# Second expert product: groups taken in neighbouring pairs, one branch for a token half around both products

## Chip, cores, metric

One core of one Trainium2 chip. The metric is the device time of one execution in microseconds; an execution also has a span, from its first to its last instruction.

## What is computed

Two blocks follow each other. The first mixes 256 tokens of width 2048; the second mixes them again and then adds a layer of experts. The change lies in the last step of that layer:

```python
act = jax.nn.gelu(jnp.einsum('thkd,td->thk', u_sel, xb))
w = (gb * act)
v_sel = expert_v[idb]
return jnp.einsum('thk,thkd->td', w, v_sel)
```

Each token takes 8 x 16 of 16384 experts; its output is the sum of their rows of `expert_v` (2048 wide), each by its weight `w`. Afterwards a last norm is taken over each token.

## The kernel before

The kernel doesn't gather rows by token. It keeps a dense table `a_dram` of weights, expert by token (zero where a token didn't choose an expert), and multiplies it with the whole of `expert_v`. It first sorts the 16384 experts into four classes: used by the first 128 tokens alone, by both halves, by the second 128 tokens alone, by nobody. `idx` holds the sorted order and `bnd` the three bounds `s1`, `e0`, `e1` between the classes (L1475 to L1514). On the inputs of the reference, its own choice of the top 16 gives classes of 3733, 6461, 3748 and 2442 experts, so `s1` = 3733, `e0` = 10194 and `e1` = 13942.

The last stage (L1525 to L1656) has its order written out by hand (`tc.manual_schedule()`, L1602). The sorted experts are cut into 64 groups of 256 (two tiles `kk` of 128). A group is loaded by four indirect DMAs on GpSimd's queue, in `v_load` and `a_load`: two 1 MB tiles `vraw` and two parts of `araw`. `v_split` (L1561) then splits each fp32 value into a high and a low part: ScalarE copies (`vh`, `ah`), VectorE subtracts (`vl`, `al`). A tile of `v` is split in two halves of 1024 columns, so a group has four half buffers of `vh` and four of `vl`; the pools hold 12 of each, three groups. `vraw` has six buffers, three groups too.

`v_mm(i, t)` (L1584) multiplies one group with one token half `t`: 24 matmuls of 512 columns (2 tiles, 4 column blocks, 3 part products), accumulated in 8 PSUM banks that stay open over all groups. For both halves a group needs two such products. A product is left out when the whole group holds no expert of that half, by branches on TensorE's sequencer (L1624 to L1629):

```python
if i < NGR - 1:
    with tc.If(e1 > lo):
        with tc.If(e0 > lo):
            v_mm(i, 0)
        with tc.If(s1 < hi):
            v_mm(i, 1)
```

Every `If` is built with an other path that waits until all matmuls issued before are done, and then raises TensorE's semaphore by what the left-out matmuls would have raised it. ScalarE waits on that semaphore before it writes a part buffer again.

The groups are taken in the order `gro` (L1541), which spreads the classes: positions 0 to 2 need both halves, position 3 is a group of unused experts with no product (an empty group), position 4 needs both, 5 the second half alone, 6 the first half alone, 7 is empty, 8 needs the second half alone, and so on. In the loop (L1612) position `i` first puts `v_split(i + 2)` on ScalarE and VectorE and the loads of `i + 4` on GpSimd, then the products of `i`. The last position (L1630) always takes both products, and the final norm and the stores follow.

Of the kernel before, what the change touches and what calls it, by code (L numbers as in the profile page):

```python
# [6 lines left out]
F32 = mybir.dt.float32  # L7
F32R = mybir.dt.float32r
# [57 lines left out]
def model(tc, I, out):  # L66
    nc = tc.nc
    V, S, T, PO = nc.vector, nc.scalar, nc.tensor, nc.gpsimd
    es = ExitStack()
    with es:  # L70
# [50 lines left out]
        def load(n):  # L121
            for hf in range(2):
                load_half(n, hf)
# [243 lines left out]
        with ExitStack() as b1:  # L367
            w_ = b1.enter_context(tc.tile_pool(name="work1", bufs=1))
# [439 lines left out]
            for u in range(4):  # L808
                t = H("xr")
                xr.append(t)  # L810
                if u < 2:
                    f = rawp.tile([128, 1024], F32, name="raw", tag="raw")
                    h, l = whp.tile([128, 1024], F32R, name="wh"), wlp.tile([128, 1024], F32R, name="wl")
# [89 lines left out]
            late = []  # L903
# [9 lines left out]
        with ExitStack() as b2:  # L913
            hb2 = b2.enter_context(tc.tile_pool(name="hb2", bufs=8, reuse_waits="tile"))
            w_ = b2.enter_context(tc.tile_pool(name="work2", bufs=1, reuse_waits="tile"))
# [205 lines left out]
        with ExitStack() as bt:  # L1121
            w_ = bt.enter_context(tc.tile_pool(name="topk", bufs=1, reuse_waits="tile"))
# [167 lines left out]
            n = len(units) + 1  # L1290
# [245 lines left out]
        w_ = es_d.enter_context(tc.tile_pool(name="vph", bufs=1, reuse_waits="tile"))  # L1536
        arow = a_dram.rearrange("p j t -> (p j) t")
        KG = 2
        NV = 12
        NGR = NT // KG  # L1540
        gro = [(i * 23 + 55) % NGR for i in range(NGR)]  # L1541
        gro[0], gro[7] = gro[7], gro[0]
        raw, ar, sv, sa = {}, {}, {}, {}

        def ix(i, kk):
# [3 lines left out]
        def v_load(i):  # L1549
            raw[i] = []  # L1550
            for kk in range(KG):
                f = w_.tile([128, 2048], F32, name="vraw", tag="vraw", bufs=6)
                PO.indirect_dma_start(f, None, I["v"], ix(i, kk))  # L1553
                raw[i].append(f)

        def a_load(i):
            ar[i] = w_.tile([128, KG, 256], F32, name="araw", tag="araw", bufs=4)
            for kk in range(KG):
                PO.indirect_dma_start(ar[i][:, kk], None, arow, ix(i, kk))  # L1559

        def v_split(i, late=False):  # L1561
            h = w_.tile([128, KG, 256], F32R, name="ah", tag="ah", bufs=3)
            l = w_.tile([128, KG, 256], F32R, name="al", tag="al", bufs=3)
            sa[i] = (h, l)
            sv[i] = []

            def a_split():
                f = ar.pop(i)
                S.activation(h, f, AF.Copy)
                V.tensor_sub(l, f, h.bitcast(F32))  # L1570

            if not late:
                a_split()
            for f in raw.pop(i):
                for hf in range(2):
                    q = slice(hf * 1024, hf * 1024 + 1024)
                    wh, wl = (w_.tile([128, 1024], F32R, name=n, tag=n, bufs=NV) for n in ("vh", "vl"))
                    S.activation(wh, f[:, q], AF.Copy)  # L1578
                    V.tensor_sub(wl, f[:, q], wh.bitcast(F32))  # L1579
                    sv[i].append((wh, wl))  # L1580
            if late:
                a_split()

        def v_mm(i, t, last=False):  # L1584
            ah, al = (x[:, :, t * 128:t * 128 + 128] for x in sa[i])

            def one(kk, d, stop):
                wh, wl = (w[:, d % 2 * 512:d % 2 * 512 + 512] for w in sv[i][kk * 2 + d // 2])
                T.matmul(ps[t][d], ah[:, kk], wh, start=False, stop=False)  # L1589
                T.matmul(ps[t][d], ah[:, kk], wl, start=False, stop=False)  # L1590
                T.matmul(ps[t][d], al[:, kk], wh, start=False, stop=stop)  # L1591

            if last:
                for d in range(4):
                    for kk in range(KG):
                        one(kk, d, kk == KG - 1)
            else:
                for kk in range(KG):
                    for d in range(4):
                        one(kk, d, False)  # L1600
# [3 lines left out]
        for i in range(3):  # L1604
            v_load(i)
            a_load(i)
        s1, e0, e1 = (T.value_load(bnd[0:1, i:i + 1], min_val=0, max_val=NT * 128) for i in range(3))
        for i in range(2):
            v_split(i, late=i == 0)
        v_load(3)  # L1610
        a_load(3)
        for i in range(NGR):  # L1612
            if i + 2 < NGR:
                v_split(i + 2)
            if i + 4 < NGR:
                v_load(i + 4)
                a_load(i + 4)
            if i + 4 == NGR:
                gl = w_.tile([128, 2048], F32, name="gl", tag="vraw", bufs=6)
                nc.sync.dma_start(gl, I["last_g"])  # L1620
                ys = [w_.tile([128, 2048], F32, name="y", tag="vraw", bufs=6) for _ in range(2)]
            lo = gro[i] * KG * 128
            hi = lo + KG * 128
            if i < NGR - 1:  # L1624
                with tc.If(e1 > lo):
                    with tc.If(e0 > lo):
                        v_mm(i, 0)
                    with tc.If(s1 < hi):  # L1628
                        v_mm(i, 1)  # L1629
            else:  # L1630
                S.preload_act_table_set("sqrt_and_others")
                sq8 = pers.tile([128, 2, 4], F32, name="sq8")
                rf = pers.tile([128, 2], F32, name="rf")
                ov = out.rearrange("(t p) d -> p t d", p=128)
                for t in range(2):
                    v_mm(i, t, last=True)
                    y = [ys[t][:, d * 512:d * 512 + 512] for d in range(4)]
                    g = [gl[:, d * 512:d * 512 + 512] for d in range(4)]
                    sq = w_.tile([128, 512], F32, name="sq", tag="sq", bufs=2)
                    for d in range(4):  # L1640
                        S.activation(sq, ps[t][d], AF.Square, accum_out=sq8[:, t, d:d + 1])  # L1641
                        if d < 3:
                            V.tensor_mul(y[d], ps[t][d], g[d])
                    r = rf[:, t:t + 1]
                    V.tensor_reduce(r, sq8[:, t], axis=AX.X, op=OP.add)  # L1645
                    S.activation(r, r, AF.Sqrt, scale=1.0 / D_MODEL, bias=eps)  # L1646
                    V.reciprocal(r, r)  # L1647
                    S.activation(y[1], y[1], AF.Copy, scale=r)
                    V.scalar_tensor_tensor(y[3], ps[t][3], r, g[3], op0=OP.mult, op1=OP.mult)  # L1649
                    nc.sync.dma_start(ov[:, t, 3 * 512:4 * 512], y[3])  # L1650
                    nc.scalar.dma_start(ov[:, t, 512:1024], y[1])
                    for c in (0, 2):
                        V.tensor_scalar(y[c], y[c], r, None, op0=OP.mult)  # L1653
                        (nc.scalar if c else nc.sync).dma_start(ov[:, t, c * 512:(c + 1) * 512], y[c])  # L1654
            sv.pop(i)
            sa.pop(i)  # L1656
    return


# [104 lines left out]
```

## Time and profile before

| | us |
|---|---|
| runs, median of 3 | 2616.54 (2615.02 to 2618.34) |
| profiled execution, its time | 2615.54 |
| its span | 2613.8 |
| last stage, first to last product matmul | 2133.1 to 2605.0 of the span |
| TensorE busy in the span | 2531.6 (97%) |
| VectorE busy | 1935.7 (74%) |
| ScalarE busy | 1491.1 (57%) |
| GpSimd busy | 708.6 (27%) |

Between the span and the execution's own time lie 1.7 us. Matmuls overlap one another in the trace: what one costs in a row of them is the distance between starts, not its duration. Times in the rows further down are counted from the span's start. Engines are PE (TensorE), PEld (its weight loads), DVE (VectorE), ACT (ScalarE), POOL (GpSimd), and PEq is TensorE's sequencer.

### The profile page before, as it was taken

The numbers are of one execution on the slowest core, as the hardware profiler recorded it, in microseconds if no ns is written. First come the engines' busy times: TensorE is split into PE (matmuls) and PEld (weight loads), VectorE is DVE, ScalarE is ACT, GpSimd is POOL, SyncE is SP. The second block draws the span as 40 slices with busy tenths as digits, with TensorE's granted clock in tenths as the row PEclk, the third lists the DMA queues.
The fourth block names the chain that finished last, engine by engine and source line by source line (L and its number), as shares of the span: only waits on it lengthen the run. The fifth ranks groups of instructions, "written<-read, shape, count | busy, mean of one in ns | idle before, by whom it ended". The sixth has DMA issues, their size and how long they took to land. (4 is left out here: it accounts for less than half of the span.)

```text
span 2613.8 us, 38685 instructions
## 1 busy us (share of the span) xinstructions
PE 2531.6 (97%) x14650; PEld 2155.8 (82%) x14650; DVE 1935.7 (74%) x2671; ACT 1491.1 (57%) x2179; POOL 708.6 (27%) x419
## 2 busy tenths in 40 slices
PE   8999999999999999999998999999999999999998
PEld 7878878888888888888887788888888877777776
DVE  7988877676556555776889988888987448767676
ACT  7666665555544544555544766666455446656565
POOL 0450111000000000001446321211322248767773
PEclk9999999999999999999999999999999999999999
DMA  6444424555554455555555577667999859988885
GB/s 222 164 165 148 162 100 145 189 172 175 169 169 166 166 187 186 184 193 195 173 197 177 191 252 242 228 229 254 354 367 329 302 202 365 350 319 324 321 309 208
DMA packets 173540, 584.80 MB, mean 224 GB/s; under 512 B 17440, under 2 KB 50976, under 8 KB 156832
## 3 DMA queue, kind: packets, MB, share of 16 engines
q1 hardware_dynamic: 114336, 411.88, 45.9%
q0 software_dynamic: 24576, 151.01, 15.7%
q10 hardware_dynamic: 34432, 19.27, 2.5%
q8 instruction: 126, 2.06, 0.3%
q14 instruction: 70, 0.57, 0.1%
HBM read 536.48 MB, written 45.61 MB: 223 GB/s over the span
## 5 line engine op out<-in xcount | busy, mean ns | idle before, releaser
L238 PE MATMUL acc<-a,wh 128*128 128x512 f32 x3106 | 1112.2, 399 | 0.6 <-DVE y L248 0.6
L239 PE MATMUL acc<-a,wl 128*128 128x256 f32 x3106 | 878.5, 283 | 16.6 <-DVE wl L118 12.4
L238 PEld LDWEIGHTS acc<-a,wh 128*128 128x128 f32 x3106 | 585.4, 189 | 128.9 <-PE acc L236 0.9
L118 DVE TENSOR_TENSOR wl<-raw,wh 128x1024 fp32r<-128x1024 f32 x372 | 463.2, 1247 | 231.2 <-ACT wh L117 228.0
L117 ACT ACTIVATE wh<-raw 128x1024 fp32r<-128x1024 f32 x414 | 437.3, 1058 | 310.2 <-PE acc L238 191.0
L239 PEld LDWEIGHTS acc<-a,wl 128*128 128x128 f32 x3106 | 589.1, 190 | 25.1 <-DVE wl L118 15.2
L118 POOL TENSOR_TENSOR wl<-raw,wh 128x1024 fp32r<-128x1024 f32 x42 | 113.0, 2691 | 1079.3 <-ACT wh L117 1038.9
L118 POOL TENSOR_TENSOR wl<-ring,wh 128x1024 fp32r<-128x1024 f32 x70 | 204.5, 2921 | 544.6 <-ACT wh L117 514.5
L117 ACT ACTIVATE wh<-ring 128x1024 fp32r<-128x1024 f32 x248 | 259.9, 1054 | 143.6 <-PE acc L238 97.7
L1579 DVE TENSOR_TENSOR vl<-vraw,vh 128x1024 fp32r<-128x1024 f32 x256 | 296.6, 1221 | 19.3 <-ACT vh L1578 14.2
L118 DVE TENSOR_TENSOR wl<-ring,wh 128x1024 fp32r<-128x1024 f32 x178 | 233.4, 1317 | 59.8 <-ACT wh L117 58.5
L238 PE MATMUL acc<-ax,wh 128*128 128x512 f32 x720 | 264.9, 406 | 11.4 <-ACT wh L822 7.3
L1589 PE MATMUL o<-vh,ah 128*128 128x512 f32 x648 | 256.2, 395 | 18.4 <-PEq L1628 7.2
L1591 PE MATMUL o<-vh,al 128*128 128x512 f32 x648 | 252.5, 390 | 2.6 <-DVE al L1570 2.6
L1590 PE MATMUL o<-vl,ah 128*128 128x512 f32 x648 | 252.2, 389 | 0.0
L1578 ACT ACTIVATE vh<-vraw 128x1024 fp32r<-128x1024 f32 x256 | 248.9, 1044 | 0.0
L239 PE MATMUL acc<-ax,wl 128*128 128x256 f32 x720 | 209.2, 291 | 5.3 <-DVE wl L118 3.1
L247 ACT ACTIVATE y<-acc 128x512 f32<-128x512 f32 x161 | 95.3, 593 | 204.3 <-PE acc L236 188.2
L248 DVE TENSOR_TENSOR y<-y,acc 128x512 f32<-128x512 f32 x161 | 110.1, 685 | 115.8 <-ACT y L247 114.9
L1559 POOL DMA_INDIRECT araw<-a_dram,idx x128 | 178.5, 1394 | 47.5 <-issue 38.1
L1553 POOL DMA_INDIRECT vraw<-in_v_dram,idx x128 | 159.2, 1244 | 78.4 <-DVE vl L1579 40.3
L238 PEld LDWEIGHTS acc<-ax,wh 128*128 128x128 f32 x720 | 138.1, 192 | 40.8 <-ACT wh L822 7.3
(516 smaller groups left out, 4044.1 us busy)
## 6 DMA issues: line engine op xcount, KB each, us to landing
raw<-in_w_dram SPq DMA_DIRECT2D x278, 512.0 KB, 4.2
ring<-in_uT_dram SPq DMA_DIRECT2D x248, 512.0 KB, 5.1
raw<-in_wo_dram SPq DMA_DIRECT2D x64, 512.0 KB, 4.4
raw<-in_wq_dram SPq DMA_DIRECT2D x32, 512.0 KB, 4.2
g_dram<-gst ACTq DMA_DIRECT2D x32, 512.0 KB, 7.4
G<-g_dram SPq DMA_DIRECT2D x32, 512.0 KB, 7.6
xs<-y SPq DMA_DIRECT2D x19, 512.0 KB, 3.9
Xr<-xs SPq DMA_DIRECT2D x19, 512.0 KB, 9.3
```

The source lines that it names most:

```text
L117: S.activation(h[:, q], f[:, q], AF.Copy)
L118: (PO if (n, hf) in POOL_SUB else V).tensor_sub(l[:, q], f[:, q], h[:, q].bitcast(F32))
L238: T.matmul(acc[:, j], wh[:, js], xx, start=f, stop=False)
L239: T.matmul(acc[:, j, 0], wl[:, js], xx[:, 0], start=False, stop=False)
L248: V.tensor_add(y, y, acc[:, :, 0])
L1553: PO.indirect_dma_start(f, None, I["v"], ix(i, kk))
L1559: PO.indirect_dma_start(ar[i][:, kk], None, arow, ix(i, kk))
L1578: S.activation(wh, f[:, q], AF.Copy)
L1579: V.tensor_sub(wl, f[:, q], wh.bitcast(F32))
L1589: T.matmul(ps[t][d], ah[:, kk], wh, start=False, stop=False)
L1590: T.matmul(ps[t][d], ah[:, kk], wl, start=False, stop=False)
L1591: T.matmul(ps[t][d], al[:, kk], wh, start=False, stop=stop)
```

## The change

The 64 groups are taken as 32 pairs of neighbours (512 sorted experts), in the order `two`. For a pair `u`, `u + 1` an outer branch asks whether the pair holds a used expert. Inside, one branch asks for the first token half and holds the products of both groups (the second under a branch of its own), and one asks for the second half in the same way, so the order of a full pair is (u, first half), (u + 1, first half), (u, second half), (u + 1, second half). The splits of the next pair stand ahead of the products but for the second tile of its second group, which stands behind them; `vh` and `vl` get 14 half buffers, `ah` and `al` four in place of three. The second group's own test against `e1` is gone.

```diff
@@ -1536,10 +1536,11 @@
         w_ = es_d.enter_context(tc.tile_pool(name="vph", bufs=1, reuse_waits="tile"))
         arow = a_dram.rearrange("p j t -> (p j) t")
         KG = 2
-        NV = 12
+        NV = 14
         NGR = NT // KG
-        gro = [(i * 23 + 55) % NGR for i in range(NGR)]
-        gro[0], gro[7] = gro[7], gro[0]
+        two = [(i * 11 + 27) % (NGR // 2) for i in range(NGR // 2)]
+        two[0], two[8] = two[8], two[0]
+        gro = [p * 2 + j for p in two for j in range(2)]
         raw, ar, sv, sa = {}, {}, {}, {}
 
         def ix(i, kk):
@@ -1558,26 +1559,28 @@
             for kk in range(KG):
                 PO.indirect_dma_start(ar[i][:, kk], None, arow, ix(i, kk))
 
-        def v_split(i, late=False):
-            h = w_.tile([128, KG, 256], F32R, name="ah", tag="ah", bufs=3)
-            l = w_.tile([128, KG, 256], F32R, name="al", tag="al", bufs=3)
-            sa[i] = (h, l)
-            sv[i] = []
-
+        def v_split(i, tiles=range(KG), late=False):
             def a_split():
                 f = ar.pop(i)
+                h, l = sa[i]
                 S.activation(h, f, AF.Copy)
                 V.tensor_sub(l, f, h.bitcast(F32))
 
-            if not late:
-                a_split()
-            for f in raw.pop(i):
+            if tiles[0] == 0:
+                sa[i] = tuple(w_.tile([128, KG, 256], F32R, name=n, tag=n, bufs=4) for n in ("ah", "al"))
+                sv[i] = []
+                if not late:
+                    a_split()
+            for kk in tiles:
+                f = raw[i][kk]
                 for hf in range(2):
                     q = slice(hf * 1024, hf * 1024 + 1024)
                     wh, wl = (w_.tile([128, 1024], F32R, name=n, tag=n, bufs=NV) for n in ("vh", "vl"))
                     S.activation(wh, f[:, q], AF.Copy)
                     V.tensor_sub(wl, f[:, q], wh.bitcast(F32))
                     sv[i].append((wh, wl))
+            if tiles[-1] == KG - 1:
+                raw.pop(i)
             if late:
                 a_split()
 
@@ -1605,29 +1608,44 @@
             v_load(i)
             a_load(i)
         s1, e0, e1 = (T.value_load(bnd[0:1, i:i + 1], min_val=0, max_val=NT * 128) for i in range(3))
+        def load(i):
+            if i < NGR:
+                v_load(i)
+                a_load(i)
+
         for i in range(2):
             v_split(i, late=i == 0)
-        v_load(3)
-        a_load(3)
-        for i in range(NGR):
-            if i + 2 < NGR:
-                v_split(i + 2)
-            if i + 4 < NGR:
-                v_load(i + 4)
-                a_load(i + 4)
-            if i + 4 == NGR:
-                gl = w_.tile([128, 2048], F32, name="gl", tag="vraw", bufs=6)
-                nc.sync.dma_start(gl, I["last_g"])
-                ys = [w_.tile([128, 2048], F32, name="y", tag="vraw", bufs=6) for _ in range(2)]
-            lo = gro[i] * KG * 128
-            hi = lo + KG * 128
-            if i < NGR - 1:
+        load(3)
+        load(4)
+        for u in range(0, NGR, 2):
+            if u + 2 < NGR:
+                v_split(u + 2)
+                load(u + 5)
+                v_split(u + 3, range(1))
+            lo = gro[u] * KG * 128
+            mid, hi = lo + KG * 128, lo + 2 * KG * 128
+            if u + 2 < NGR:
                 with tc.If(e1 > lo):
                     with tc.If(e0 > lo):
-                        v_mm(i, 0)
+                        v_mm(u, 0)
+                        with tc.If(e0 > mid):
+                            v_mm(u + 1, 0)
                     with tc.If(s1 < hi):
-                        v_mm(i, 1)
+                        with tc.If(s1 < mid):
+                            v_mm(u, 1)
+                        v_mm(u + 1, 1)
+                v_split(u + 3, range(1, 2))
+                load(u + 6)
+                if u + 4 == NGR:
+                    gl = w_.tile([128, 2048], F32, name="gl", tag="vraw", bufs=6)
+                    nc.sync.dma_start(gl, I["last_g"])
+                    ys = [w_.tile([128, 2048], F32, name="y", tag="vraw", bufs=6) for _ in range(2)]
             else:
+                with tc.If(e0 > lo):
+                    v_mm(u, 0)
+                with tc.If(s1 < mid):
+                    v_mm(u, 1)
+                i = u + 1
                 S.preload_act_table_set("sqrt_and_others")
                 sq8 = pers.tile([128, 2, 4], F32, name="sq8")
                 rf = pers.tile([128, 2], F32, name="rf")
@@ -1652,8 +1670,9 @@
                     for c in (0, 2):
                         V.tensor_scalar(y[c], y[c], r, None, op0=OP.mult)
                         (nc.scalar if c else nc.sync).dma_start(ov[:, t, c * 512:(c + 1) * 512], y[c])
-            sv.pop(i)
-            sa.pop(i)
+            for i in range(u, u + 2):
+                sv.pop(i)
+                sa.pop(i)
     return
```

The built program is the same up to TensorE's first branch of the stage. Behind it the order differs on ScalarE, at two places. In the names, `vh_`, `ah_` are the high parts written, `vraw_`, `araw_` the loaded tiles; in brackets are the semaphores waited for (DMASW: a load, DVE: VectorE, PE: TensorE).

The first place is ScalarE where the products of an empty position are passed. Before, around position 3 (`ah_20905` is position 4, `ah_20983` position 5):

```order
L1569 ACTIVATE ah_20905<-araw_20773 128x512 [waits DMASW2_49,DMASW3_49,DVE_49,PE_49]
L1578 ACTIVATE vh_20909<-vraw_20769 128x1024 [waits DMASW0_49,DVE_49,PE_49]
L1578 ACTIVATE vh_20913<-vraw_20769 128x1024
L1578 ACTIVATE vh_20917<-vraw_20771 128x1024 [waits DMASW1_49]
L1578 ACTIVATE vh_20921<-vraw_20771 128x1024
L1625 UNCONDITIONAL_BRANCH
L1569 ACTIVATE ah_20983<-araw_20851 128x512 [waits DMASW6_49,DMASW7_49,DVE_49,PE_49]
```

Each position waits for TensorE once, at its start, for the position three before it.

After, around the first empty pair (positions 6 and 7; `vh_21206` and `vh_21210` are the second tile of position 7, `ah_21221` to `vh_21237` position 8, `ah_21248` to `vh_21365` position 9):

```order
L1579 ACTIVATE vh_21206<-vraw_20933 128x1024 [waits DMASW5_49,DVE_49,PE_49]
L1579 ACTIVATE vh_21210<-vraw_20933 128x1024
L1628 UNCONDITIONAL_BRANCH
L1566 ACTIVATE ah_21221<-araw_21063 128x512 [waits DMASW3_49,DMASW2_49]
L1579 ACTIVATE vh_21225<-vraw_21059 128x1024 [waits DMASW0_49]
L1579 ACTIVATE vh_21229<-vraw_21059 128x1024
L1579 ACTIVATE vh_21233<-vraw_21061 128x1024 [waits DMASW1_49]
L1579 ACTIVATE vh_21237<-vraw_21061 128x1024
L1566 ACTIVATE ah_21248<-araw_21090 128x512 [waits DMASW7_49,DMASW6_49]
L1579 ACTIVATE vh_21252<-vraw_21086 128x1024 [waits DMASW4_49]
L1579 ACTIVATE vh_21256<-vraw_21086 128x1024
L1579 ACTIVATE vh_21361<-vraw_21088 128x1024 [waits DMASW5_49,DVE_49,PE_49]
```

ScalarE now waits for TensorE once in a pair, at the second tile of the pair's second group: `vh_21206` waits for the end of the whole pair of positions 4 and 5, and all of positions 8 and 9 stand behind it.

The second place is the start of the stage on ScalarE. After (`ah_20702` is position 0, `ah_20722` position 1):

```order
L1579 ACTIVATE vh_20704<-vraw_20654 128x1024 [waits DMASW0_49]
L1579 ACTIVATE vh_20708<-vraw_20654 128x1024
L1579 ACTIVATE vh_20712<-vraw_20656 128x1024 [waits DMAHW6_49,DMAHW0_49,DMAHW7_49,DMASW1_49,DVE_49]
L1579 ACTIVATE vh_20716<-vraw_20656 128x1024 [waits PE_49]
L1566 ACTIVATE ah_20702<-araw_20658 128x512 [waits DMASW3_49,DMASW2_49]
L1566 ACTIVATE ah_20722<-araw_20665 128x512 [waits DMASW7_49,DMASW6_49]
```

Before, the order of positions 0 and 1 was the same there, but none of these copies waited for TensorE; VectorE's first subtraction did. On TensorE the second product is now that of position 1, where it was the second half of position 0.

## Rows read from the trace of the kernel before

**Rows 1.** Groups by line, last stage: line, engine, tiles, count | busy, mean ns | idle before.
```profile
L1589 PE MATMUL o<-vh,ah 128*128 128x512 f32 x648 | 256.2, 395 | 18.4 <-PEq L1628 7.2 <-PEq L1626 5.8 <-ACT ah L1569 3.7
```
**Rows 2.** A stretch of the last stage: busy time (count) of each engine, PEclk, DMA share, GB/s.
```profile
2190.00:2210.00 20.00, 17.68 (x77) 14.01 (x76) 16.21 (x16) 13.49 (x16) 15.83 (x13) 1.00 1.00 382
```
**Rows 3.** Who waited for whom, last stage: us in total, times, longest.
```profile
ACT ah L1569 <- PE o L1590: 127.8, 32, 7.1
```
**Rows 4.** Timeline of PE: start, us, instruction [idle before <-releaser]; first run and last matmul.
```profile
2136.75 0.39 PE L1589 MATMUL o<-vh,ah 128*128 128x512 f32 x1
...
2168.51 0.39 PE L1591 MATMUL o<-vh,al 128*128 128x512 f32 x1
...
2605.04 0.39 PE L1591 MATMUL o<-vh,al 128*128 128x512 f32 x1
```
**Rows 5.** Timeline of PE: first matmul behind each left-out product.
```profile
2169.34 0.49 PE L1589 MATMUL o<-vh,ah 128*128 128x512 f32 x1 [0.44 <-ACT ah L1569]
...
2180.80 0.49 PE L1589 MATMUL o<-vh,ah 128*128 128x512 f32 x1 [0.32 <-PEq L1626]
...
2193.61 0.49 PE L1589 MATMUL o<-vh,ah 128*128 128x512 f32 x1 [1.65 <-PEq L1626]
...
2205.45 0.49 PE L1589 MATMUL o<-vh,ah 128*128 128x512 f32 x1 [0.67 <-PEq L1628]
...
2228.78 0.49 PE L1589 MATMUL o<-vh,ah 128*128 128x512 f32 x1 [0.68 <-ACT vh L1578]
...
2240.39 0.49 PE L1589 MATMUL o<-vh,ah 128*128 128x512 f32 x1 [0.44 <-ACT ah L1569]
```
**Rows 6.** Timeline of ACT and DVE: the splits behind a release by PE.
```profile
2168.71 0.63 ACT L1569 ACTIVATE ah<-araw 128x512 fp32r<-128x512 f32 x1 [3.92 <-PE o L1590]
2169.25 3.89 ACT L1578 ACTIVATE vh<-vraw 128x1024 fp32r<-128x1024 f32 x4
...
2170.32 4.68 DVE L1579 TENSOR_TENSOR vl<-vraw,vh 128x1024 fp32r<-128x1024 f32 x4 [0.26 <-ACT vh L1578]
...
2174.93 0.68 DVE L1570 TENSOR_TENSOR al<-araw,ah 128x512 fp32r<-128x512 f32 x1
2175.53 4.62 DVE L1579 TENSOR_TENSOR vl<-vraw,vh 128x1024 fp32r<-128x1024 f32 x4
```
**Rows 7.** Groups by line, last stage, DVE.
```profile
L1579 DVE TENSOR_TENSOR vl<-vraw,vh 128x1024 fp32r<-128x1024 f32 x256 | 296.6, 1221 | 19.3 <-ACT vh L1578 14.2 <-PE o L1532 4.9 <-DMA vraw<-in_v_dram,idx 0.3
```
**Rows 8.** Timelines of the start of the stage: PE and DVE.
```profile
2136.42 0.50 PE L1591 MATMUL o<-vh,al 128*128 128x512 f32 x1 [2.63 <-DVE al L1570]
...
2142.70 4.63 DVE L1579 TENSOR_TENSOR vl<-vraw,vh 128x1024 fp32r<-128x1024 f32 x4 [0.26 <-ACT vh L1578]
```
**Rows 9.** Timeline of PE around a long wait in an earlier stage.
```profile
1410.89 0.58 PE L239 MATMUL acc<-a,wl 128*128 128x256 f32 x1 [4.85 <-DVE wl L118]
1411.27 0.63 PE L238 MATMUL acc<-a,wh 128*128 128x512 f32 x1
...
1414.47 0.60 PE L238 MATMUL acc<-a,wh 128*128 128x512 f32 x1
...
1416.19 0.40 PE L238 MATMUL acc<-a,wh 128*128 128x512 f32 x1
...
1419.66 0.39 PE L238 MATMUL acc<-a,wh 128*128 128x512 f32 x1
```
**Rows 10.** Stretches around the waits of rows 9 and rows 8, columns as in rows 2.
```profile
1406.00:1411.00 5.00, 0.15 (x2) 0.12 (x1) 5.00 (x3) 1.38 (x2) 5.00 (x2) 0.71 0.00 0
1411.00:1413.00 2.00, 2.00 (x7) 1.71 (x8) 2.00 (x2) 0.00 (x0) 2.00 (x1) 0.50 0.47 135
1413.00:1415.00 2.00, 2.00 (x8) 1.71 (x7) 2.00 (x3) 0.00 (x0) 0.06 (x1) 0.52 0.97 334
1415.00:1419.00 4.00, 4.00 (x26) 3.50 (x25) 4.00 (x3) 2.72 (x3) 0.00 (x0) 1.00 0.86 302
...
2137.00:2141.00 4.00, 4.00 (x19) 3.31 (x18) 0.00 (x0) 0.00 (x0) 3.01 (x4) 1.00 0.92 350
```

## Prediction

> **What bounds the kernel now.** Up to the last stage the built program stays the same, so only that stage is read. First the groups of PE: 648 matmuls of each of three lines [rows 1], 24 to a product, so 3 x 648 / 24 = 81 products. The rules of the branches, applied to the class bounds 3733, 10194 and 13942, give 81 as well, so those bounds can be used to say what each `If` does. Then PE's timeline: in an unbroken run 140 steps from 2136.75 to 2168.51 take 31.76 us [rows 4], 0.227 us a matmul, 5.45 us a product. From the late start at 2136.42 [rows 8] to the last matmul at 2605.04 [rows 4] lie 468.6 us for 1941 steps, which need 440.6: 28.0 us are lost, and they lie at the places where a product is left out. PE is the bound; these losses and PE's own work are all that the change can shift.
>
> The price of one place comes from the 48 matmuls (10.90 us) that follow one start and end at the next [rows 5]. Passing an empty group: 2228.78 to 2240.39, 0.71 us. Leaving out the first token half ahead of a second one: 2169.34 to 2180.80, 0.56. Leaving out the second half at a group's end: 2193.61 to 2205.45, 0.94. Three in a row (second half, empty group, first half): 2180.80 to 2193.61, 1.91. Between groups that both need both halves nothing is lost: the run of 141 matmuls [rows 4] crosses five such borders. The cause is in the code: the other path of an `If` waits until PE has drained.
>
> What feeds PE must keep up. VectorE needs 1.22 us for a half of a tile [rows 7], and ScalarE waits for PE to release buffers, 127.8 us in 32 waits [rows 3]; in the early part the loads take the whole of the DMA engines [rows 2].
>
> **The pairs.** By the class bounds the 32 pairs are of four kinds: A, all four products (13 pairs); B, both groups with the first half only (7); C, with the second half only (8); E, empty (4). In order: A B A E A A E A C E A C E A, then C B A six times. That is 13 x 4 + 15 x 2 = 82 products, one more than before: pair 27 holds groups 54 and 55, `e1` lies in 54, and the test that skipped 55 by itself is gone.
>
> **The change part by part.**
> - *Left-out products.* All 28.0 us go, and these come back. Eight C at 0.56; each passes one more compare, which I bound by 0 and 0.38 (0.94 less 0.56: the skip at the end passes a jump and two compares more) and take as a third, 0.13: 5.5 us. Seven B at 0.94: 6.6 us. Between C and B nothing is lost, nor in A. The pair of groups 14 and 15 and that of 38 and 39 hold a bound and stay A.
> - *The added product.* 24 x 0.227 = 5.4 us on PE, on the path.
> - *The empty pairs.* This is the large term. While PE works on the pair ahead of an empty one, the 14 half buffers hold: eight of that pair, and four and two of the empty pair. ScalarE next waits for the end of the pair (the wait at the second tile of the second group), and the split of the pair behind the empty one stands behind that wait, and with it VectorE's subtractions and the loads that wait for those. An empty pair gives PE nothing to do meanwhile, so PE waits for: two halves of the empty pair, `ah`, then the first half it needs. ScalarE's earlier release came at 2168.71 from the last matmul but one, which with the pitch puts the release by the last one 0.2 us after the next matmul could have started. VectorE begins 1.07 us behind ScalarE (2169.25 to 2170.32); a half goes every 1.17 us (4.68 / 4), `al` takes 0.60, the last half 1.22 [rows 6, 7]. So the first `vl` is there 0.2 + 1.07 + 2.34 + 0.60 + 1.22 = 5.4 us after PE ran out, and PE's second matmul, due at 0.2, waits for it: 5.2 us, four times, 20.8 us. After that PE takes 6 x 0.227 = 1.36 us to a half and VectorE 1.17, so nothing more is late. Bounds for one: 0.71, the price of an empty group [rows 5], and 6.4, if the load of the next group is a microsecond late. I take 5.2, since the chain consists of measured steps. Before, this wait didn't exist: the split of the position behind an empty one waited for the group two positions ahead of the empty one, which had long ended.
> - *The clock behind such a wait.* [...] There two matmuls took 0.64 us (five pairs from 1411.27 to 1414.47) against 0.347 (ten pairs from 1416.19 to 1419.66) [rows 9]: in 3.9 us 46% are lost, 1.8 us. Behind the wait of 2.63 us at 2136.42 [rows 8] the clock stayed at 1.00 [rows 10]. The new waits, with one matmul within them, are nearer to 4.85, so I take 1.8 us at each of four, 7.2 us; bounds 0 and 9.0 (the start as well).
> - *The start.* The second product is now that of position 1, whose first `vl` is there at 2142.70 + 1.22 = 2143.9 [rows 8]; PE's second matmul waits for that, so the product begins as if at 2143.8. Before, the second product began at 2136.42 + 22 x 0.227 = 2141.4. Loss 2.4 us. That `vl` of position 0 no longer waits for PE brings the first product forward and nothing else.
> - *Loads and queues.* GpSimd issues the same loads in the same order; each load waits for the subtraction three groups ahead, as before. The ten subtractions of a pair take VectorE 8 x 1.22 + 2 x 0.68 = 11.1 us [rows 6, 7], against 10.9 us for a pair with two products; the A that follows every such couple gives the time back. That cover holds as long as a pair of two products isn't followed by two more.
>
> Sum: -28.0 + 5.5 + 6.6 + 5.4 + 20.8 + 7.2 + 2.4 = +19.9 us. The profiled execution took 2615.5 us, 1.0 less than the median of the runs; set on the median 2616.5, the forecast is **2636 us**. A measurement of this kernel tells 0.2%, 5.2 us, from no change.
>
> **A rule against the change.** A longer body means a longer jump. The rows show no price for length: passing an empty group jumps over twice the code of a left-out half and costs 0.71 against 0.56 [rows 5]. [...]
>
> **Rivals.**
> - *The clock stays up* behind the four waits: the single matmul within each could be enough. For it: the 2.63 us that left the clock alone. Then 2636 - 7.2 = 2629 us.
> - *The splits get ahead*, not slower: if the part buffers behind an empty pair came free before the pair ahead of it ends, its four waits would shrink to 0.71 each. Place: ScalarE's one wait in a pair. It decides when that wait is met by the third of four products already, 5.45 us earlier. Then -28.0 + 5.5 + 6.6 + 5.4 + 2.8 + 2.4 = -5.3, 2611 us, right at the border of faster. Against it: the wait stands behind the whole pair, and before, ScalarE's 32 waits ended at the last matmuls of a group [rows 3].
> [...]
>
> **How the numbers follow.** Forecast 0.60, clock stays up 0.20, splits get ahead 0.08, fetch 0.06, and 0.06 for a mixture that ends near the old time. The range takes the first two with their bounds: low 2618 (waits of 3.5 us, the middle between their bounds, and no loss of clock: 2629 less 6.8, less 4 for a start without loss and cheaper skips), high 2646 (waits of 6.4, clock lost at the start too, dearer compares: 4.8 + 1.8 + 2.0 over 2636, rounded up). Faster by over 0.2%: half of the second rival and a little of the rest, 0.06. Within 0.2%: 0.08. Slower: 0.86.
>
> **What would show it.** Right: 656 matmuls of each product line; four waits of PE of about 5 us for `vl` or `ah`, each behind a pair of four or two products, with granted clock near 0.5 for some 4 us behind them; 15 short gaps of 0.5 to 1 us; first to last product matmul some 492 us instead of 472. Wrong: gaps at the empty pairs below 2 us, or a clock of 1.00 behind them (then 7 us less), or gaps of 2 us at every skip.

## The result, and the profile after

| | before | after |
|---|---|---|
| median | 2615.72 us (2615.02 to 2618.34, 5 runs) | 2642.84 us (2637.47 to 2644.72, 5 runs) |
| profiled execution | 2615.54 us | 2637.47 us |

The ratio is 1.0097 [1.0086, 1.0108]: the change makes the kernel 1% slower. The forecast was 2636 us, its range 2618 to 2646.

The profiled execution is the shortest of the five, so first a common zero for both traces. The stage begins behind 64 identity matmuls (L1532), which no branch or split of the change touches. Their summary lines give the first and the last start, before:

```profile
L1532 PE MATMUL o<-cst,x x64: 275/275/377, 2125.4 to 2132.5; 128*128 128x128 f32 x64
```

and after:

```profile
L1532 PE MATMUL o<-cst,x x64: 275/275/377, 2121.6 to 2128.7; 128*128 128x128 f32 x64
```

Up to here the program is the same, and this execution came 3.8 us earlier. From there to the last product matmul, at 2605.04 [rows 4] and at 2627.18, lie 472.5 and 498.5 us. The stage grew by 26.0 us, and the 21.9 us between the two profiled times are 26.0 less 3.8 and, after rounding, some 0.2 behind the stage. This distance, called **stage time**, stands below beside the medians.

Groups by line of the stage after, PE and ACT, to be read against [rows 1]:

```profile
L1592 PE MATMUL o<-vh,ah 128*128 128x512 f32 x656 | 262.9, 401 | 27.7 <-ACT vh L1579 20.5 <-PEq L1629 3.5 <-PEq L1633 2.7
...
L1566 ACT ACTIVATE ah<-araw 128x512 fp32r<-128x512 f32 x64 | 39.9, 623 | 87.7 <-DMA araw<-a_dram,idx 87.7
```

656 matmuls a line are 82 products, as forecast. The idle time of PE used to end with the sequencer (PEq); now most of it ends with a split on ScalarE. The waits of ScalarE, after, against [rows 3]:

```profile
ACT vh L1579 <- PE o L1594: 111.8, 20, 13.0
```

20 waits for a release in place of 32, and the release is now met in `vh` and not in `ah`: it is the second tile of the pair's second group. What that does shows at the first empty pair. From here on a gap in the text is the distance between two starts less the 0.23 us that a matmul takes in a row; the idle time in brackets, which counts from the end of a matmul, is smaller. PE's timeline there, and the last matmul:

```profile
2193.39 0.39 PE L1594 MATMUL o<-vh,al 128*128 128x512 f32 x1
2197.34 0.80 PE L1592 MATMUL o<-vh,ah 128*128 128x512 f32 x1 [3.56 <-ACT vh L1579]
2199.05 0.80 PE L1593 MATMUL o<-vl,ah 128*128 128x512 f32 x1 [0.92 <-DVE vl L1580]
2199.65 0.63 PE L1594 MATMUL o<-vh,al 128*128 128x512 f32 x1
2200.07 0.63 PE L1592 MATMUL o<-vh,ah 128*128 128x512 f32 x1
...
2627.18 0.39 PE L1594 MATMUL o<-vh,al 128*128 128x512 f32 x1
```

ACT's timeline in the same stretch:

```profile
2193.82 2.00 ACT L1579 ACTIVATE vh<-vraw 128x1024 fp32r<-128x1024 f32 x2 [10.98 <-PE o L1594]
2195.72 0.61 ACT L1566 ACTIVATE ah<-araw 128x512 fp32r<-128x512 f32 x1
2196.24 3.88 ACT L1579 ACTIVATE vh<-vraw 128x1024 fp32r<-128x1024 f32 x4
```

and DVE's:

```profile
2194.90 2.36 DVE L1580 TENSOR_TENSOR vl<-vraw,vh 128x1024 fp32r<-128x1024 f32 x2 [10.62 <-ACT vh L1579]
2197.18 0.68 DVE L1567 TENSOR_TENSOR al<-araw,ah 128x512 fp32r<-128x512 f32 x1
2197.78 4.62 DVE L1580 TENSOR_TENSOR vl<-vraw,vh 128x1024 fp32r<-128x1024 f32 x4
```

The pair ahead ends at 2193.4. ScalarE had idled 11 us for that; now it splits the two halves that the empty pair still lacks, then `ah`, then the first half that PE needs. PE's second matmul starts at 2199.05, 5.66 us behind the last one of the pair, of which 0.23 + 0.23 would have passed anyway: 5.2 us lost. Then each matmul takes 0.43 us, until 2204. The granted clock in stretches ahead, within and behind (columns as in [rows 2]):

```profile
2186.00:2190.00 4.00, 4.00 (x20) 3.30 (x19) 0.00 (x0) 0.00 (x0) 3.09 (x4) 1.00 0.96 339
2193.50:2197.00 3.50, 0.28 (x2) 0.00 (x0) 2.10 (x2) 3.19 (x4) 0.00 (x0) 1.00 0.52 212
2197.00:2199.00 2.00, 0.80 (x1) 0.29 (x1) 2.00 (x4) 2.00 (x3) 1.16 (x2) 0.58 0.00 0
2199.00:2204.00 5.00, 4.95 (x12) 3.89 (x13) 5.00 (x5) 5.00 (x7) 4.39 (x3) 0.50 0.65 241
2204.00:2206.00 2.00, 2.00 (x10) 1.66 (x9) 2.00 (x3) 1.33 (x3) 1.70 (x2) 0.96 0.42 107
...
2141.00:2146.00 5.00, 4.54 (x12) 3.48 (x12) 4.60 (x5) 3.67 (x6) 4.09 (x3) 0.50 1.02 418
```

At a granted 0.50 the matmuls stand 0.42 to 0.43 us apart (2199.65 to 2200.07 in the rows above); at 1.00 they stand 0.23 apart.

The other three empty pairs look the same: restarts at 2248.58, 2289.64 and 2330.69 with first gaps of 3.72 us, and granted clocks of 0.50 to 0.53 in the 4.5 to 5 us from the second matmul on. The last row of the windows is the start of the stage, where the clock fell too. PE's timeline there:

```profile
2135.65 0.39 PE L1594 MATMUL o<-vh,al 128*128 128x512 f32 x1
2140.29 0.80 PE L1592 MATMUL o<-vh,ah 128*128 128x512 f32 x1 [4.26 <-ACT vh L1579]
2141.55 0.79 PE L1593 MATMUL o<-vl,ah 128*128 128x512 f32 x1 [0.46 <-DVE vl L1580]
```

What PE waited for is the high part of position 1, and ScalarE's `ah` of position 1 waited for its load, before (first line) and after:

```profile
2141.08 0.63 ACT L1569 ACTIVATE ah<-araw 128x512 fp32r<-128x512 f32 x1 [8.08 <-DMA araw<-a_dram,idx]
...
2138.66 0.63 ACT L1566 ACTIVATE ah<-araw 128x512 fp32r<-128x512 f32 x1 [8.73 <-DMA araw<-a_dram,idx]
```

Last, two ordinary skips, the first half left out (C) and the second (B):

```profile
2274.91 0.49 PE L1592 MATMUL o<-vh,ah 128*128 128x512 f32 x1 [0.44 <-PEq L1629]
2379.69 0.49 PE L1592 MATMUL o<-vh,ah 128*128 128x512 f32 x1 [0.67 <-ACT vh L1579]
```

### The profile page after: what moved, and what is told of

Same layout as the page of the kernel before. It is cut to its first block, busy times and chain, and to the rows that moved or that the text cites. A ratio compares the mean times of both kernels' runs of the same rounds, so it can differ in the third digit from the quotient of the medians.

```text
span 2635.7 us, 38519 instructions
## 1 busy us (share of the span) xinstructions
PE 2544.9 (97%) x14674; PEld 2170.3 (82%) x14674; DVE 1930.9 (73%) x2671; ACT 1490.3 (57%) x2179; POOL 716.6 (27%) x419
## 3 DMA queue, kind: packets, MB, share of 16 engines
q8 instruction: 125, 2.05, 0.3%
## 5 line engine op out<-in xcount | busy, mean ns | idle before, releaser
L1592 PE MATMUL o<-vh,ah 128*128 128x512 f32 x656 | 262.9, 401 | 27.7 <-ACT vh L1579 20.5
L1593 PE MATMUL o<-vl,ah 128*128 128x512 f32 x656 | 260.9, 398 | 4.2 <-DVE vl L1580 4.2
L1594 PE MATMUL o<-vh,al 128*128 128x512 f32 x656 | 260.1, 396 | 0.0
L1554 POOL DMA_INDIRECT vraw<-in_v_dram,idx x128 | 169.8, 1327 | 102.5 <-DVE vl L1580 64.7
L1560 POOL DMA_INDIRECT araw<-a_dram,idx x128 | 172.5, 1348 | 47.6 <-issue 35.4
L1592 PEld LDWEIGHTS o<-vh,ah 128*128 128x128 f32 x656 | 126.4, 193 | 62.3 <-ACT vh L1579 26.0
```

## The experiments

The theory: the four empty pairs cost a wait for the splits each, because 14 half buffers are all held until the pair ahead ends as a whole, and a stretch at half clock; these 30 us outweigh what the branches save. Stage time runs from the last identity matmul to the last product matmul of each profiled run, so it is one value a row; where the changed kernel's stage time is compared, it is 498.1 us, the mean of its two. The ratio is taken to runs of the kernel before beside it, whose medians lay between 2615.7 and 2618.8 us.

| run | median us | ratio to before, 95% | stage us |
|---|---|---|---|
| before | | | 472.5 |
| after | 2642.84 | 1.0097 [1.0086, 1.0108] | 498.5 |
| after, again | 2641.00 | 1.0084 [1.0071, 1.0097] | 497.7 |
| own test for the second group | 2639.86 | 1.0086 [1.0073, 1.0099] | 497.6 |
| no empty pairs | 2609.99 | 0.9967 [0.9956, 0.9979] | 467.5 |
| zeros in the wait | 2636.35 | 1.0070 [1.0057, 1.0083] | 491.9 |
| 16 half buffers, 5 load buffers | 2640.33 | 1.0090 [1.0076, 1.0105] | 495.8 |
| before with 14 half buffers | 2615.68 | 0.9994 [0.9986, 1.0003] | 471.1 |
| first pair as singles | 2632.71 | 1.0061 [1.0046, 1.0076] | 491.7 |
| singles ahead of empty pairs | 2628.42 | 1.0050 [1.0035, 1.0064] | 483.6 |
| single empty units | 2604.71 | 0.9950 [0.9937, 0.9962] | 463.9 |
| the same, other order | 2603.80 | 0.9951 [0.9938, 0.9965] | 462.1 |

### The changed kernel once more

> The changed kernel once more, unchanged. Its five runs lay between 2637.5 and 2644.7 us, and the profiled one was the shortest. Theory: the four waits behind the empty pairs are about 5.5 us each in every run, and the runs differ by how long the granted clock stays at 0.50 behind them; so 2637 to 2645 again, and in a profile nearer to 2643 the segments behind the waits lose more than 2.0 us. Rival: the runs differ somewhere ahead of the product stage, as those of the kernel before do (2615.0 to 2618.3); then the product stage has 497 us again whatever the total is.

Measured: 2638.36 to 2641.70 us. The profiled run took 2641.70, and its stage time was 497.7 us, within 1 us of the other's although the whole run was 4.2 us longer; in the 22 matmuls behind the first slow one 1.84 to 2.02 us were lost at each wait, no more than in the first profile (2.05 to 2.14). So the rival holds: the runs differ ahead of the stage. Its last identity matmul started at 2133.7, not 2128.7.

### Before with 14 half buffers

```diff
-        NV = 12
+        NV = 14
```

> The kernel before with 14 half buffers of parts instead of 12, nothing else. Theory: the buffers alone do nothing, since PE never waited for a split behind the start; 2616 us, within 0.2%, and the same 28 us lost at left-out products. Rival: ScalarE and VectorE run further ahead and the start or the waits on release gain, 2 to 3 us less.

Measured: 2615.68 us against 2616.41 of the kernel before beside it: no difference in the medians, as the theory said. The stage was 1.4 us shorter in this one profile, and that stands at the start: the third product matmul came 2.6 us behind the last identity matmul, where it came 3.9 behind it before. That is less than the rival's 2 to 3 us.

### No empty pairs

```diff
+        two = [p for p in two if p < 28]
+        NGR = 2 * len(two)
```

> The changed kernel without the four empty pairs: groups 56 to 63, which no product uses with these inputs, are neither loaded nor split nor visited. Theory: the four waits of 5.5 us and the four stretches at half clock behind them (2.0 us each) go, 30 us: 2613 us, no gap over 2 us after the start, clock 1.00 from 2150 on. Rival (the loss sits in the clock or in the loads, not in ScalarE's one release a pair): a third or more of the 30 us stays, since PE then waits at other pairs, for the loads that the empty pairs gave time for; above 2622 us.

Measured: 31.0 us less than the changed kernel on the same chip (2641.0), 30.6 in stage time, and behind the start no gap over 0.91 us. PE's group there:

```profile
L1594 PE MATMUL o<-vh,ah 128*128 128x512 f32 x656 | 257.8, 393 | 13.6 <-ACT vh L1581 5.6 <-PEq L1631 3.8 <-PEq L1635 2.6
```

The loss goes with the empty pairs. That the kernel is now faster than before (0.9967), though 82 products run and the start still waits, isn't a like comparison: the kernel before passes the eight groups that are left out here, at 0.71 us each [rows 5] an estimated 5.7 us, and this stage is 5.0 us shorter than its. So the run shows what the empty pairs cost, and no gain by the pairs' branches.

### A test of its own for the second group

```diff
-                        v_mm(u + 1, 1)
+                        with tc.If(e1 > mid):
+                            v_mm(u + 1, 1)
```

> The changed kernel with a test of its own for the second group of a pair again (e1 > mid around the last product), so that group 55 is passed over. Theory: the added product costs PE's own time on the path, 24 x 0.227 = 5.4 us, less some 0.6 us for the new skip: 4.8 us less than the changed kernel, 648 matmuls of each line; the other pairs pass one compare more, which costs nothing where the branch isn't taken. Rival: that product stands beside a wait and is hidden, then no change; or compares in the way cost 0.1 us in each of 27 pairs, then 2 us of it go.

Measured: 1.1 us less in the median, 0.1 to 0.9 in stage time; the rival, not the 4.8 us. The pair that lost its product stands right ahead of an empty pair, and the wait grew from 3.7 to 8.1 us. DVE, from the release by the pair ahead on:

```profile
2275.46 2.36 DVE L1580 TENSOR_TENSOR vl<-vraw,vh 128x1024 fp32r<-128x1024 f32 x2 [4.80 <-issue]
2277.74 0.69 DVE L1567 TENSOR_TENSOR al<-araw,ah 128x512 fp32r<-128x512 f32 x1
2278.34 4.62 DVE L1580 TENSOR_TENSOR vl<-vraw,vh 128x1024 fp32r<-128x1024 f32 x4
2282.88 0.68 DVE L1567 TENSOR_TENSOR al<-araw,ah 128x512 fp32r<-128x512 f32 x1
2283.48 4.62 DVE L1580 TENSOR_TENSOR vl<-vraw,vh 128x1024 fp32r<-128x1024 f32 x4
2288.02 0.69 DVE L1567 TENSOR_TENSOR al<-araw,ah 128x512 fp32r<-128x512 f32 x1
```

and PE:

```profile
2288.46 0.79 PE L1592 MATMUL o<-vh,ah 128*128 128x512 f32 x1 [7.96 <-ACT vh L1579]
2289.90 0.79 PE L1593 MATMUL o<-vl,ah 128*128 128x512 f32 x1 [0.65 <-DVE vl L1580]
```

VectorE subtracts without a pause from 2275.5 on. Counted from the restart behind the second empty pair, PE ran out 5.6 us earlier than in the changed kernel, but its second matmul could start only 1.5 us earlier, and most of that was lost again at half clock (0.50 from 2288 to 2296) and at a further wait of 0.5 us. The added product stands beside VectorE's work.

### Zeros in the wait

```diff
+        zz = w_.tile([128, 512], F32R, name="zz", tag="zz", bufs=1)
+        V.memset(zz.bitcast(F32), 0.0)
...
+                if gro[u] >= 56:
+                    for _ in range(4):
+                        for d in range(4):
+                            T.matmul(ps[0][d], zz[:, 0:128], zz, start=False, stop=False)
                 v_split(u + 3, range(1, 2))
```

> The changed kernel with 16 matmuls of a tile of zeros (128x512, added to the first token half's sums, which they leave as they are) behind each empty pair, 16 x 0.227 = 3.6 us, in which PE otherwise waits. Theory: the granted clock falls because PE stands still, so it stays at 1.00 and the 2.0 us lost behind each wait come back: 8 us less than the changed kernel, while the waits themselves still end at the same time (gaps of some 0.2 and 1.5 us where 3.7 and 1.5 stood). Rival: the clock falls for another reason (or 16 matmuls of zeros do not hold it), then 0.50 behind the waits as before and no change; the fill delays PE, then up to 4 x 0.3 us more.

Measured: 4.7 us less than the 2641.0 in the median, 6.2 in stage time. PE at the first empty pair:

```profile
2196.14 0.39 PE L1594 MATMUL o<-vh,al 128*128 128x512 f32 x1
2196.68 3.89 PE L1642 MATMUL o<-zz 128*128 128x512 f32 x16
2200.41 0.39 PE L1592 MATMUL o<-vh,ah 128*128 128x512 f32 x1
2201.82 0.50 PE L1593 MATMUL o<-vl,ah 128*128 128x512 f32 x1 [1.02 <-DVE vl L1580]
```

The clock there, and behind the third empty pair:

```profile
2202.00:2206.00 4.00, 4.00 (x18) 3.31 (x19) 4.00 (x5) 4.00 (x5) 3.69 (x2) 1.00 0.82 295
...
2292.00:2296.00 4.00, 4.00 (x13) 3.15 (x12) 2.94 (x4) 2.26 (x3) 3.31 (x3) 0.63 1.07 424
```

The second matmul starts 5.68 us behind the pair ahead, as without zeros (5.66), and then runs at full clock. So it is at the second and the fourth: behind the second matmuls there, at 2250.69 and 2330.66, PE takes 0.34 us for one step and 0.22 to 0.24 for each of the next ones, where 0.43 stood. At these three the half clock goes when PE has work within the wait, and it is a cost apart from the wait. At the third the second matmul started 6.5 us behind the pair ahead, PE stood idle for 0.8 us behind the zeros and for 0.8 ahead of the second matmul, and 1.7 us were lost all the same; hence 6 us and not 8.

### 16 half buffers, 5 load buffers

```diff
-        NV = 14
+        NV = 16
-    ... tag="vraw", bufs=6)
+    ... tag="vraw", bufs=5)
```

> The changed kernel with 16 half buffers of parts instead of 14, and 5 load buffers instead of 6 to make room. Theory: with 16 ScalarE has split the whole empty pair before the pair ahead of it ends, so behind the release only ah and the first half of the next pair stand: the wait shrinks by two halves, 2 x 1.17 us, from 5.5 to some 3.1 us, four times 2.4 = 9.5 us, and with it perhaps part of the half clock (bounds 0 and 8): 2625 to 2633 us. Rival (the wait is set by the loads behind the empty pair): nothing gained, and with one load buffer less the waits grow; 2643 us or more.

Measured: no gain in all, and both theory and rival in one trace. Behind the first two empty pairs the wait is the 3.1 us of the theory (2202.05 to 2205.14, where 5.66 stood):

```profile
2203.88 0.49 PE L1592 MATMUL o<-vh,ah 128*128 128x512 f32 x1 [1.44 <-ACT vh L1579]
2205.14 0.50 PE L1593 MATMUL o<-vl,ah 128*128 128x512 f32 x1 [0.77 <-DVE vl L1580]
```

Ahead of the third, ACT waits for loads at each position:

```profile
2271.11 0.63 ACT L1566 ACTIVATE ah<-araw 128x512 fp32r<-128x512 f32 x1 [6.38 <-DMA araw<-a_dram,idx]
...
2284.02 0.63 ACT L1566 ACTIVATE ah<-araw 128x512 fp32r<-128x512 f32 x1 [2.25 <-DMA araw<-a_dram,idx]
```

Between these two stands one more, 1.80 us, at 2277.34: a position comes every 6.2 to 6.9 us, at a DMA share of 0.97 to 1.02 from 2270 to 2280, and PE's first gap at the third empty pair grew to 6.4 us. The start lost another 3 us: the second load was issued 6 us later, counted from the last identity matmul, where it waited for products of the stage ahead (PE acc L219). What two buffers of parts gave, the missing load buffer took. 16 half buffers with six load buffers weren't tried.

### The first pair as single units

```diff
-    ... (38, 2), (12, 2), ...
+    ... (38, 1), (39, 1), (12, 2), ...
```

From here on the units are a list of (first group, groups); a single unit has the branches of the kernel before, and the splits reach seven tiles ahead of a unit's start, as in the changed kernel. The diffs of these runs are shortened to the list.

> The changed kernel, but its first pair (groups 38 and 39) run as two single units, so that both first products read position 0; the order of groups and the splits ahead stay. Theory: from the last identity matmul (line L1532) to the unbroken run, the changed kernel loses 9.4 us (1.3 until the first product, gaps of 4.4, 1.0 and 0.4, 2.3 at a lower clock), where 2.4 more than the 3.6 of the kernel before were forecast; with position 0's second product in between position 1 is split in time and some 5.5 us come back: 2635 to 2636 us. Rival: position 1 is late by its load whatever stands ahead, then the wait comes one product later and is as long less 5.4 us, and the gain is the same, but a gap of 1 us or more stays at the 49th product matmul.

Measured: 6.4 us less in stage time; by the ratios (1.0084 to 1.0061) 6.0, in the medians 8.3 less than the changed kernel's 2641.0. The gaps of 4.4 and 1.0 us are gone; one of 0.85 us remains at the 50th matmul. Position 1's load was no earlier (its `ah` began 10.8 us behind the last identity matmul, 9.95 in the changed kernel), which is what the rival said, though the gap is under its 1 us. The four waits behind the empty pairs stayed as they were: 3.72 us, then 1.49 to 1.53.

### Single units ahead of the empty pairs

```diff
-    ... (34, 2), (56, 2), ... (36, 2), (58, 2), ... (54, 2), (60, 2), ... (40, 2), (62, 2), ...
+    ... (34, 1), (35, 1), (56, 2), ... (36, 1), (37, 1), (58, 2), ... (54, 1), (55, 1), (60, 2), ... (40, 1), (41, 1), (62, 2), ...
```

> The changed kernel, but each of the four pairs ahead of an empty pair runs as two single units (groups 34, 35, 36, 37, 54, 55, 40, 41); the order, the empty pairs and the 14 half buffers stay. Group 55 is passed over by its own unit. Theory (the wait comes from the pair's one release): ScalarE is then released by the first of the two units already, the empty pair is split before the second one ends, and the waits behind the first two empty pairs go from 5.5 us and 2.0 at half clock to about 0.8: 13 us less. Behind the third and fourth, with little work of PE ahead, the loads (about 6.5 us a position at a DMA share of 1.0) are the next bound: anything between 0.8 and 5 us there, 0 to 13 us less. In all 2615 to 2628 us. Rival (an empty pair costs its own splits, however the releases stand): gaps of 5 us at all four, 2641 us.

Measured: 2628.42 us in the median, at the upper end of what was expected (2615 to 2628), and 483.6 us of stage time, 14.5 less. PE at the first empty pair, and its first matmul behind the second:

```profile
2191.96 0.39 PE L1596 MATMUL o<-vh,al 128*128 128x512 f32 x1
2192.84 0.49 PE L1594 MATMUL o<-vh,ah 128*128 128x512 f32 x1 [0.49 <-PEq L1645]
...
2237.07 0.49 PE L1594 MATMUL o<-vh,ah 128*128 128x512 f32 x1 [0.44 <-ACT ah L1568]
```

The waits of 5.2 us have become gaps of 0.65 and 0.60 us. The empty pairs are the same; only the pairs ahead of them are cut in two, and with them the releases. The loop over units isn't it: the run with the first pair as single units has the same loop, and its four waits stayed. That settles the cause at these two: it is the one release per pair. At the third and fourth empty pair gaps of 7.1 and 3.4 us stayed. At the third, three empty groups (55, 60, 61) stand behind a single product, and VectorE subtracts from 2260.2 to 2278 without a pause. So there the splits of three groups, not the loads that the expectation named, are the next bound. At the fourth it is the loads, as expected. ScalarE's `ah` waited for one:

```profile
2313.85 0.63 ACT L1568 ACTIVATE ah<-araw 128x512 fp32r<-128x512 f32 x1 [2.58 <-DMA araw<-a_dram,idx]
```

PE's first matmul could start only at 2315.48.

### Single empty units, in two orders

```diff
-        two = [(i * 11 + 27) % (NGR // 2) for i in range(NGR // 2)]
-        two[0], two[8] = two[8], two[0]
-        gro = [p * 2 + j for p in two for j in range(2)]
+        units_ = [(38, 1), (39, 1), (14, 2), (0, 2), (16, 2), (40, 2), (18, 2), (55, 1), (42, 2), (20, 2), (2, 2),
+                  ...
+                  (54, 1), (10, 2), (63, 1), (52, 2), (12, 2), (32, 2)]
+        gro = [g + j for g, n in units_ for j in range(n)]
```

> Pairs for groups 0 to 37 and 40 to 53 only; groups 54 to 63 are single units, of which no two stand together, and the first two units are the groups 38 and 39 as singles, so that the first two products both read position 0. 14 half buffers, splits up to seven tiles ahead of a unit's start. Theory: an empty single unit leaves the first two halves of the next position split, so PE loses the branch alone: nine times 0.71 = 6.4, seven B at 0.84 = 5.9, seven C at 0.60 = 4.2, group 54 0.6, and no start loss: 17 us where the kernel before loses 28, with 81 products: 2616 - 11 = 2605 us, clock 1.00 throughout, faster than both. Rival: a wait for a release or for loads comes at the empty units again (1 to 3 us each and half clock behind them), then 2616 or more.

Measured: 2604.71 us, as expected, and a stage time of 463.9 us, 8.6 less than before. The first ten products run without a gap. One wait was left near the end, behind a short pair, an empty unit and a short pair in a row:

```profile
2560.59 0.49 PE L1594 MATMUL o<-vh,ah 128*128 128x512 f32 x1 [1.15 <-ACT vh L1581]
2561.84 0.50 PE L1595 MATMUL o<-vl,ah 128*128 128x512 f32 x1 [0.77 <-DVE vl L1582]
```

The other order was to take that wait away:

> The version of single empty units (x_mix) in another order: the short units are spread so that no stretch needs loads faster than about 7 us a position. Theory: the one wait that was left there (1.3 and 1.0 us and 1.7 us of clock near the end, behind B, an empty unit and C in a row) goes: 4 us less, some 2601 us, with losses of 17 us at branches alone. Rival: the order that starts with five short pairs after one long puts the loads behind early, and waits of 1 to 3 us come there: 2605 us or more.

Measured: 2603.80 us and a stage time of 462.1. The wait is gone, but one of 1.4 us came at the third product. In the medians the two can't be told apart (0.9950 and 0.9951). Both are faster than both kernels: 0.5% under before, 1.4% under the changed one. They change several things at once (the start, the empty units, the tests of groups 54 and 55, the order), so they show that such a mix is faster, not what each of these is worth.

## Why the prediction was right, and where its sum was off

Stage time went up by 26.0 us, where the sum was +19.9.

| term | forecast | measured |
|---|---|---|
| losses before, gone | -28.0 | -28.0 |
| eight C | 5.5 | 5.6 (gaps of 0.60, and 0.1 in the run behind each) |
| seven B | 6.6 | 6.3 (gaps of 0.70 to 0.91, and some 0.1 behind each) |
| the 82nd product | 5.4 | 5.4, but see below |
| four waits behind empty pairs | 20.8 | 20.9 (3.72 + 1.49 to 1.52 each) |
| clock behind them | 7.2 | 9.8 |
| the start | 2.4 | 5.9 |
| sum | 19.9 | 25.9 |

- **Left-out products.** The price of 0.56 + 0.13 us for a C was right: 0.60 and 0.1.
- **The empty pairs.** The chain of release, two halves, `ah`, first half came out to a tenth of a microsecond, and its cause, one release per pair, is shown at the first two by the run with single units ahead of them; that the loss goes with the empty pairs, by the run without them.
- **The clock.** This term was mis-sized, with the mechanism right. The share lost was as forecast (0.20 of 0.43 us, where 46% was taken), but the forecast had 3.9 us at half clock, as in the earlier stage (0.50 and 0.52 from 1411 to 1415 [rows 10]), and here it lasted 5 us from the second matmul on, 2199 to 2204: 0.37 us were lost at the first matmul and 2.0 to 2.1 in the run that follows, 2.4 to 2.5 a time. The zeros show that it is a cost apart from the wait.
- **The start.** This term was mis-sized most. It took the time of position 1's first `vl` (2143.9) from the trace before, 11.4 us behind the last identity matmul; after, PE's matmul on it started 12.85 us behind (2141.55 less 2128.7), since ScalarE's wait for position 1's load ended 1.4 us later, counted in this way (9.95 us behind the last identity matmul, 8.53 before). The pairs need not be the reason: in the profile of the kernel before with 14 half buffers it ended 9.8 us behind. What made it later is open. The clock fell behind this wait too, 2.3 us, which the sum had only in its upper bound. Together that is most of what was missing: by the 60th product matmul the start had cost 5.9 us more than before, 3.5 over the forecast. As single units the first pair gave 6.4 us of stage time back.
- **The added product.** It was put on the path with its full 5.4 us. As bookkeeping that holds, with the wait behind it at 5.2; as a cost that one could take back it doesn't: without it the wait grew by 4.4 us, and 0.1 to 0.9 us of stage time came of it. That step failed: a term that stands ahead of a wait for another engine is not on the path by itself.
- **Loads and queues.** In the changed kernel nothing more was late behind the start, as said. But the cover was thin: at the third empty pair VectorE's splits (own test, single units) or the loads (5 load buffers) took over, at the fourth the loads (single units).
- **Rivals.** *The clock stays up*: it fell at all four waits (0.50 to 0.53) and at the start (0.50); it took zeros within the wait to keep it up, at three of the four. *The splits get ahead*: not here, yet with single units ahead it is just what happened, with 0.65 us at the first empty pair, near the 0.71 priced. *Longer jumps cost more* (the 0.06 called fetch): no run shows it. Skips over two products take 0.60 and 0.83 us, and in the run with single units a jump over a whole empty pair, four products, is within the 0.65 us.

The median lies 7 us over the forecast: 6 from the two terms above (the start 3.5, the clock 2.6), the rest within the spread of the runs. So the forecast came out in its range by its mechanism: the wait, its largest new term, measured 20.9 against 20.8. The 5.4 us of the added product fit only as bookkeeping.

## What to carry over

When branches or loops are merged into larger units, the buffers that a unit holds come free in larger lots. Ask at each unit that may be empty what is split by then, and what waits for the one release; the depth must cover the largest unit and all that can be jumped behind it, or the units that can be empty must stay small and apart. And price a term beside a wait by what the other engine could deliver, not by its own length.

## What the runs showed of the hardware

- **Runs differ ahead of the stage.** In the twelve profiles the last identity matmul started between 2128.1 and 2136.0 us, although the program up to there does the same work, while the changed kernel's stage time came to 498.5 and 497.7. A stage is compared better from its own first event than from the span's start.
- **The clock behind equal gaps.** In the run with 16 half buffers PE had gaps of 1.60 and 1.03 us at both of the first two empty pairs. Behind the first it went on at 1.00, behind the second at 0.65:

```profile
2204.00:2208.00 4.00, 3.23 (x14) 2.42 (x15) 4.00 (x4) 4.00 (x5) 1.51 (x1) 1.00 0.09 37
2250.00:2254.00 4.00, 3.06 (x7) 2.27 (x8) 3.85 (x4) 4.00 (x6) 1.22 (x1) 0.65 0.64 260
```

  The kernel before had an idle time of 2.63 us with the clock at 1.00 behind it [rows 8, 10]. So the same gap can cost 0 or over 1 us (eight matmuls from 2251.43 on took 3.41 us in place of 1.8); why, these runs don't settle.
